# Seeding PSUM with the first half of a product instead of adding it afterwards

## The chip, the cores and the metric

One core of one Trainium2 chip runs the kernel. Its engines work from queues of their own and meet at semaphores: PE (TensorE) multiplies matrices into the PSUM banks, DVE (VectorE) and ACT (ScalarE) do elementwise work and read or write PSUM, POOL (GpSimd) helps with additions, SP (SyncE) issues most DMA transfers. Time is device microseconds of one execution, the median of several; lower is better.

## The reference

One inference step of two trunk layers on 576 tokens (512 of a prompt, 64 of eight sampled sequences), model width 2048, all in float32. Cut to what matters here:

```python
def trunk_layer(x, p, ...):
    h = rmsnorm(x, pre_g)
    proj = h @ w_in                                   # 2048 -> 6144 columns
    u, gp, q, k, v, gr = jnp.split(proj, SPLITS, axis=-1)
    pool_y, buf_new = pool_mixer(u, buf0, ...)        # windows 2, 4, 8, 16, then w_pool
    pool_y = pool_y * silu(gp)
    ret_y, S_new = retention(q.., k.., v.., S0, start)   # rope, 4 heads
    ret_y = head_rmsnorm(ret_y) * silu(gr)
    mix = concatenate([pool_y, ret_y]) @ w_out
    x = x + rmsnorm(mix, post_g)
    ple = rmsnorm(p @ w_ple, ple_g)
    gate = sigmoid(x @ w_ple_gate + b_ple_gate)
    x = x + gate * ple
    return x, S_new, buf_new
```

## The kernel before

**Tiling.** Everything is kept with channels on the 128 partitions and the 576 tokens (`NT`) along the free axis, as two halves of 288 (`HN`), because a PSUM bank holds 512 floats: `half(t, h)` is one half of a tile. A column is one tile of 128 output channels. A float32 product is made of three passes over parts that are split into a high and a low word: `split_part` (L86, L87) makes `wh` on ACT (a cast) and `wl` on DVE (the rest); a column with eight tiles of input is 8 x 3 x 2 = 48 matmuls (L132) into two banks of the four `acc` buffers.

**Two halves of a product.** The input projection and the gate are computed in two halves of the input channels. The first half runs through a Strassen-like scheme (`blocks`, `unit`) whose results go out to DRAM, `proj_dram` and `gate_dram`. The second half is a plain gemm of eight input tiles per column (`gemm`). Its result and the saved first half have to be added: the saved half is loaded into a `part` tile (L451 for the projection, L830 for the gate), DVE adds the two banks to it half by half (L457, L774), and the rest of the work reads the tile.

**The stages that matter.** Per layer: `in_first` (first half of the projection), `in_phase` (its second half, column pairs by `columns(pr)`, then heads of retention and groups of pooling), `out_phase`. The last begins with the output product, then ple, then the gate: its first half by `gate_step`, its second half by the loop at L826 to L835, 16 columns in 8 pairs, which I call the gate's second half. Per column `ct` it loads the saved half, splits the column's weights (two parts, each 128x512), runs the gemm, and calls `gated` (L765 to L786): load of the saved `ple` tile (L767), its scaling on DVE by an STT (scalar_tensor_tensor, L768), two half adds (L774), one sigmoid on ACT over the full width (L776), the product and the residual add on DVE (L777, L778), and a store of the column, `y` in layer 1 (L780), `x` in layer 0 (L782). In layer 0 the loop also squares each column (L314 on ACT, summed on DVE) and, for the first eight columns, scales it for the next layer (L821, in place, so after its store) and splits it again.

**What sets the order.** The code is written column by column; a scheduler lays the instructions of each engine out beforehand and the engines then run their rows strictly in that order, each row waiting for its semaphores. SP's row of DMA issues is one such order: a load that waits holds up all loads behind it. Buffers are rings by tag: `part` has 4, `x` 4 (the ple tiles), `wh` and `wl` 5 each, `raw` (1 MB of weights, one pair of columns) 2. A new tile takes the place of the oldest of its tag and waits for that tile's last reader:

```python
BUFS = {"raw": 2, "wh": 5, "wl": 5, "S": 3, "long": 4, "tmp": 4, "d": 4, "part": 4, "x": 4, "u": 6, ...}
```

So a weight load waits until the last part of the pair two earlier has been split, and a ple load until the residual add of the column four earlier has read its tile.

Of the kernel before, what the change touches and what calls it, by code (L numbers as in the profile page):

```python
# [19 lines left out]
NS = 8  # L20
# [13 lines left out]
def half(ap, h):  # L34
    return ap[:, h * HN:(h + 1) * HN]
# [3 lines left out]
def decoder_kernel(ctx: ExitStack, tc: tile.TileContext, a, decay8):  # L39
# [6 lines left out]
    def buf(tag, shape=(P, NT), dt=F32):  # L46
        return sb.tile(list(shape), dt, tag=tag, name=tag, bufs=BUFS.get(tag, 1))
# [74 lines left out]
    def bank(shape):  # L122
        return ps.tile(list(shape), F32, tag="pb", name="pb", bufs=2)

    def gemm(w, xs, new=acc_tile, by_half=False):
        acc = [new()[:, :HN] for _ in range(2)]
        n = len(w)
        for hs in ((0,), (1,)) if by_half else ((0, 1),):
            for i, ((wh, wl), (xh, xl)) in enumerate(zip(w, xs)):
                for passno, (u, v) in enumerate(((wh, xh), (wh, xl), (wl, xh))):  # L130
                    for h in hs:
                        nc.tensor.matmul(  # L132
                            acc[h], u, v[:, h * HN:(h + 1) * HN],
                            start=(i == 0 and passno == 0), stop=(i == n - 1 and passno == 2),
                        )
        return acc

# [304 lines left out]
    def in_phase(l, raws, r2, rB, cos, sin):  # L442
        b_ring, st_ring, rot_ring, s0_ring = Ring(0, 12), Ring(12, 4), Ring(16, 8), Ring(24, 4)

        def columns(pr):
            keys = [("in2", p) for p in pairs] + [("out", 0, 0), ("out", 0, 1)]
            i = keys.index(("in2", pr))
            raw = raws.pop(("in2", pr))
            for c in range(2):
                t = buf("part")  # L450
                nc.sync.dma_start(out=t, in_=proj_dram[l][2 * pr + c])  # L451
                w = split_weights(raw, 8 * c, 8)
                if c == 1:
                    fetch(l, raws, keys[i + 1:i + 3])
                acc = gemm(w, r2)
                for h in range(2):
                    nc.vector.tensor_tensor(out=half(t, h), in0=acc[h], in1=half(t, h), op=ALU.add)  # L457
                yield t

        def rotary(pr):  # L460
            x = [rot_ring.tile() for _ in range(2)]
            u = [buf("d") for _ in range(2)]
            for i, t in enumerate(columns(pr)):
                nc.vector.tensor_tensor(out=x[i], in0=t, in1=cos, op=ALU.mult)
                nc.vector.tensor_tensor(out=u[i], in0=t, in1=sin, op=ALU.mult)
            nc.vector.tensor_tensor(out=x[0], in0=x[0], in1=u[1], op=ALU.subtract)
            nc.vector.tensor_tensor(out=x[1], in0=x[1], in1=u[0], op=ALU.add)
            return x

        def silu_gates(pr):  # L470
            for t in columns(pr):
                g = buf("g")
                nc.vector.tensor_tensor(out=g, in0=t, in1=rB, op=ALU.mult)
                nc.scalar.activation(g, g, AF.Silu)
                yield g

# [56 lines left out]
        def head(h):  # L533
# [14 lines left out]
            kst = sample_rows(sample_part(k, "kdec_s", h), (0, 2))  # L548

            v = [rot_ring.tile() for _ in range(2)]  # L550
            for i, t in enumerate(columns(16 + h)):
                nc.vector.tensor_tensor(out=v[i], in0=t, in1=rB, op=ALU.mult)
            vt = token_major(v)
            vc = buf("smp", (P, 2, 64))
            for e in range(2):
# [73 lines left out]
        def pool_group(g):  # L629
            w = WINDOWS[g]  # L630
            npool = buf("np", (P, 2, 9, BUF))
            wraw = buf("u", (P, 2, DK))
            nc.sync.dma_start(out=wraw, in_=a["w_pool"][l, g])
            es = buf("u", (P, 2, NB, SEG))
            nc.sync.dma_start(out=es, in_=a["state_pool"][l, :, 2 * g:2 * g + 2])
            wh, wl = buf("u", (P, 2, DK), F32R), buf("u", (P, 2, DK), F32R)
            split(wh, wl, wraw)
            xs = []
            for i, t in enumerate(columns(g)):
                e = buf("d", (P, BUF + NP))  # L640
                nc.vector.memset(e[:, :BUF], 0.0)
                nc.vector.tensor_tensor(out=e[:, BUF:], in0=t[:, :NP], in1=rB[:, :NP], op=ALU.mult)
                nc.vector.tensor_tensor(  # L643
                    out=es[:, i, :, BUF:], in0=t[:, NP:].rearrange("p (b s) -> p b s", s=NS),
                    in1=rB[:, NP:].rearrange("p (b s) -> p b s", s=NS), op=ALU.mult,
                )
                nc.scalar.copy(npool[:, i, 0], e[:, NP:NP + BUF])
                nc.scalar.copy(npool[:, i, 1:], es[:, i, :, NS:])
                s, ss, sh = e, es[:, i], 1
                while sh < w:  # L650
                    n = tmp()[:, :BUF + NP]
                    m = buf("es", (P, NB, SEG))
                    lo = 2 * sh - 1
                    nc.gpsimd.tensor_tensor(out=n[:, lo:], in0=s[:, lo:], in1=s[:, sh - 1:BUF + NP - sh], op=ALU.add)
                    nc.gpsimd.tensor_tensor(out=m[:, :, lo:], in0=ss[:, :, lo:], in1=ss[:, :, sh - 1:SEG - sh], op=ALU.add)  # L655
                    s, ss, sh = n, m, 2 * sh
                p = tmp()
                nc.vector.tensor_tensor(out=p[:, :16], in0=s[:, BUF:BUF + 16], in1=consts["invcnt"][:, g], op=ALU.mult)
                nc.vector.tensor_tensor(out=p[:, :16], in0=p[:, :16], in1=e[:, BUF:BUF + 16], op=ALU.subtract)
                nc.vector.scalar_tensor_tensor(  # L660
                    out=p[:, 16:NP], in0=s[:, BUF + 16:], scalar=1.0 / w, in1=e[:, BUF + 16:], op0=ALU.mult, op1=ALU.subtract
                )
                nc.vector.scalar_tensor_tensor(
                    out=p[:, NP:].rearrange("p (b s) -> p b s", s=NS), in0=ss[:, :, BUF:], scalar=1.0 / w,
                    in1=es[:, i, :, BUF:], op0=ALU.mult, op1=ALU.subtract,
                )
                hi, lo = buf("u", (P, NT), F32R), buf("u", (P, NT), F32R)
                split(hi, lo, p)
                xs.append((hi, lo))
            nc.sync.dma_start(out=a["new_pool"][l, :, 2 * g:2 * g + 2], in_=npool)  # L670
            for c, gate in enumerate(silu_gates(4 + g)):
                acc = gemm([(wh[:, i, c * P:(c + 1) * P], wl[:, i, c * P:(c + 1) * P]) for i in range(2)], xs, mix_tile)
                kt = 2 * g + c
                y = buf("d")
                for i in range(2):
                    nc.vector.scalar_tensor_tensor(
                        out=half(y, i), in0=acc[i], scalar=vec["pool_scale"][:, l, kt:kt + 1], in1=half(gate, i),
                        op0=ALU.mult, op1=ALU.mult,
                    )
                nc.sync.dma_start(out=m_dram[l][kt], in_=y)  # L680
# [16 lines left out]
    def out_phase(l, raws, ops_out):  # L697
# [64 lines left out]
            stats["ss"] = buf("long")  # L762
        rP = buf("long")

        def gated(ct, t, acc, by_half):  # L765
            pl = buf("x")
            nc.sync.dma_start(out=pl, in_=ple_dram[l][ct])  # L767
            nc.vector.scalar_tensor_tensor(  # L768
                out=pl, in0=pl, scalar=vec["ple_g"][:, l, ct:ct + 1], in1=rP, op0=ALU.mult, op1=ALU.mult
            )  # L770
            for hs in ((0,), (1,)) if by_half else ((0, 1),):
                cols = slice(hs[0] * HN, (hs[-1] + 1) * HN)
                for h in hs:
                    nc.vector.tensor_tensor(out=half(t, h), in0=acc[h], in1=half(t, h), op=ALU.add)  # L774
                gate, pc, mc = t[:, cols], pl[:, cols], mo[ct][:, cols]
                nc.scalar.activation(gate, gate, AF.Sigmoid, bias=vec["b_gate"][:, l, ct:ct + 1])  # L776
                nc.vector.tensor_tensor(out=pc, in0=pc, in1=gate, op=ALU.mult)  # L777
                nc.vector.tensor_tensor(out=mc, in0=mc, in1=pc, op=ALU.add)  # L778
                if l == L - 1:
                    nc.sync.dma_start(out=a["y"][:, ct, cols], in_=mc)  # L780
            if l < L - 1:
                nc.sync.dma_start(out=x_dram[ct], in_=mo[ct])  # L782
                square_into(stats["ss"], mo[ct], ct == 0)
# [41 lines left out]
        for p in range(8):  # L825
            raw = raws.pop(("gate2", p))  # L826
            for c in range(2):
                ct = 2 * p + c
                t = buf("part")
                nc.sync.dma_start(out=t, in_=gate_dram[l][ct])  # L830
                w = split_weights(raw, 8 * c, 8)
                if c == 1:
                    fetch_gate(p + 9, p + 11)
                by_half = l == L - 1 and ct == KT - 1
                gated(ct, t, gemm(w, g2, by_half=by_half), by_half)  # L835
            if l < L - 1 and p >= 4:
                blocks(next_xs, [p - 4], next_ops, plain="d")
                if 5 <= p < 7:
# [103 lines left out]
```

## Time and profile before

| | us |
|---|---|
| median of three runs (lowest, highest) | 2267.46 (2265.41, 2268.45) |
| profiled execution, its span | 2264.7 |
| PE busy | 2238.1 |
| DVE busy | 1738.2 |
| ACT busy | 1033.5 |
| gate's second half, layer 0: first column's gemm to last | 1028.8 to 1133.6 |
| gate's second half, layer 1 | 2151.9 to 2258.5 |

The profile is of one execution; no time of that execution other than its span is given, so the span stands for it. Busy time of PE is modelled, and matmuls overlap: one of 128x288 is shown with 0.29 us while the next begins 0.13 us after it. The rows further below show idle time together with the engine or transfer that ended it; the columns are named with each group.

### The profile page before, as it was taken

How to read it: one execution, taken by the hardware profiler on the slowest of the kernel's cores; microseconds unless marked ns; L12 is line 12 of the kernel's file. 1: busy time of each engine (PE TensorE's matmuls, PEld its weight loads, DVE VectorE, ACT ScalarE, POOL GpSimd, SP SyncE). 2: the span in 40 equal slices, each digit the busy share in tenths (PEclk: the TensorE clock that was granted, in tenths of full speed). 3: DMA queues.
4: the chain of work that ended last, by engine and by line, in shares of the span. 5: the costliest groups of instructions: out<-in, count | busy, mean ns of one | idle time of the engine just before them, and what ended most of it. 6: DMA issues, size and time to landing. Idle time of an engine off the chain costs nothing.

```text
span 2264.7 us, 42491 instructions
## 1 busy us (share of the span) xinstructions
PE 2238.1 (99%) x16692; PEld 2153.5 (95%) x16692; DVE 1738.2 (77%) x3141; ACT 1033.5 (46%) x2033; POOL 173.0 (8%) x145
## 2 busy tenths in 40 slices
PE   8999999999999999999999999999999999999998
PEld 8999998898899999899999999988998999998998
DVE  8788766566589898788877786665665989988866
ACT  5465532333334555655545554333333345556532
POOL 2000000000043110000020000000001421100000
PEclk9999999999999999999999999999999999999999
DMA  6455444545343333646644444455454443335564
GB/s 221 151 192 175 156 159 140 174 143 177 127 161 135 130 125 117 215 156 208 222 153 151 164 160 160 145 165 158 135 180 143 148 151 125 115 127 197 174 205 153
DMA packets 137641, 361.92 MB, mean 160 GB/s; under 512 B 14496, under 2 KB 51808, under 8 KB 116576
## 3 DMA queue, kind: packets, MB, share of 16 engines
q1 hardware_dynamic: 137440, 359.20, 47.2%
q8 instruction: 131, 2.15, 0.4%
q14 instruction: 70, 0.57, 0.1%
HBM read 273.10 MB, written 86.04 MB: 159 GB/s over the span
## 4 chain that ended last, share of the span: by engine, by line
PE 81%; DVE 10%; DMA 5%; issue 2%; ACT 1%; SPq 0%; POOL 0%; DVEq 0%; ACTq 0%; POOLq 0%
PE acc L132 27%; PE acc L114 12%; PE acc L113 11%; PE acc L112 11%; PE acc L222 4%; DMA x<-ple 3%; PE pb L113 3%; PE pb L112 3%; PE pb L114 3%; DVE wl L87 2%; PE po L345 2%; PE pb L348 1%; PE po L288 1%; DVE m L87 1%; PE po L132 1%
## 5 line engine op out<-in xcount | busy, mean ns | idle before, releaser
L132 PE MATMUL acc<-m,wh 128*128 128x288 f32 x3584 | 648.6, 297 | 0.0
L86 ACT CAST wh<-raw 128x512 fp32r<-128x512 f32 x567 | 350.7, 619 | 560.6 <-PE acc L132 306.1
L113 PE MATMUL acc<-m,wh 128*128 128x288 f32 x1944 | 573.5, 296 | 0.0
L114 PE MATMUL acc<-m,wl 128*128 128x288 f32 x1944 | 569.0, 296 | 1.8 <-DVE wl L87 1.8
L112 PE MATMUL acc<-m,wh 128*128 128x288 f32 x1944 | 570.7, 295 | 0.0
L132 PEld LDWEIGHTS acc<-m,wh 128*128 128x128 f32 x3584 | 529.5, 188 | 13.2 <-issue 8.8
L87 DVE TENSOR_TENSOR wl<-raw,wh 128x512 fp32r<-128x512 f32 x567 | 409.2, 723 | 121.4 <-ACT wh L86 110.2
L132 PE MATMUL acc<-m,wl 128*128 128x288 f32 x1792 | 401.0, 298 | 0.0
L114 PEld LDWEIGHTS acc<-m,wl 128*128 128x128 f32 x1944 | 363.2, 188 | 2.9 <-DVE wl L87 2.7
L113 PEld LDWEIGHTS acc<-m,wh 128*128 128x128 f32 x1944 | 365.3, 188 | 0.0
L112 PEld LDWEIGHTS acc<-m,wh 128*128 128x128 f32 x1944 | 364.6, 188 | 0.6 <-issue 0.2
L86 ACT CAST wh<-S 128x512 fp32r<-128x512 f32 x356 | 220.6, 620 | 238.1 <-PE acc L113 135.1
L132 PEld LDWEIGHTS acc<-m,wl 128*128 128x128 f32 x1792 | 291.1, 188 | 9.7 <-issue 6.7
L87 DVE TENSOR_TENSOR wl<-S,wh 128x512 fp32r<-128x512 f32 x356 | 252.3, 709 | 29.9 <-ACT wh L86 28.2
L457 DVE TENSOR_TENSOR part<-acc,part 128x288 f32<-128x288 f32 x192 | 79.2, 450 | 64.4 <-PE acc L132 62.8
L235 POOL TENSOR_TENSOR S<-raw 128x512 f32<-128x512 f32 x45 | 67.5, 1499 | 684.4 <-DVE wl L87 316.5
L655 POOL TENSOR_TENSOR es<-u 128x176 f32<-128x176 f32 x16 | 14.5, 908 | 1112.4 <-DVE u L643 1112.2
L235 DVE TENSOR_TENSOR S<-raw 128x512 f32<-128x512 f32 x133 | 91.5, 688 | 9.3 <-DMA raw<-in_w_in 7.2
L349 DVE SCALAR_TENSOR_TENSOR m<-m,pb 128x512 f32<-128x512 f32 x64 | 43.3, 686 | 70.9 <-PE po L345 43.4
L113 PE MATMUL pb<-m,wh 128*128 128x288 f32 x324 | 95.6, 295 | 0.0
L112 PE MATMUL pb<-m,wh 128*128 128x288 f32 x324 | 95.2, 294 | 0.0
L114 PE MATMUL pb<-m,wl 128*128 128x288 f32 x324 | 95.1, 294 | 0.0
(262 smaller groups left out, 3479.6 us busy)
## 6 DMA issues: line engine op xcount, KB each, us to landing
raw<-in_w_in SPq DMA_DIRECT2D x95, 1024.0 KB, 5.3
raw<-in_w_out SPq DMA_DIRECT2D x32, 1024.0 KB, 5.0
raw<-in_w_gate SPq DMA_DIRECT2D x32, 1024.0 KB, 5.5
proj<-d SPq DMA_DIRECT2D x96, 288.0 KB, 2.1
part<-proj SPq DMA_DIRECT2D x96, 288.0 KB, 2.8
m<-in_state_ret SPq DMA_DIRECT2D x64, 256.0 KB, 3.0
out_new_ret_s<-m SPq DMA_DIRECT2D x64, 256.0 KB, 2.8
x<-m SPq DMA_DIRECT2D x48, 288.0 KB, 3.0
```

The lines of the kernel that those rows point to most:

```text
L86: nc.scalar.copy(hi, src)
L87: return nc.vector.tensor_tensor(out=lo, in0=src, in1=hi.bitcast(F32), op=ALU.subtract)
L112: nc.tensor.matmul(out, wh, xh, start=start, stop=False, **kw)
L113: nc.tensor.matmul(out, wh, xl, start=False, stop=False, **kw)
L114: nc.tensor.matmul(out, wl, xh, start=False, stop=stop, **kw)
L132: nc.tensor.matmul(acc[h], u, v[:, h * HN:(h + 1) * HN], start=(i == 0 and passno == 0), stop=(i == n - 1 and passno == 2),)
L222: nc.tensor.matmul(acc[h], w[:, j], xs[h][passno == 1], start=(i == 0 and j == 0 and passno == 0), stop=(i == 1 and j == 3 and passno == 2),)
L235: eng.tensor_tensor(out=s, in0=x, in1=y, op=op)
L288: nc.tensor.matmul(sums[32 * q:32 * q + 32], ones, src[:, q * QN:(q + 1) * QN], start=start, stop=stop)
L345: nc.tensor.matmul(po_s[rows, bg], qrep[:, dt, b * 32:b * 32 + 32], s0[:, dt], start=(dt == 0), stop=(dt == 1))
L349: nc.vector.scalar_tensor_tensor(out=s0, in0=s0, scalar=decay8[h], in1=sp, op0=ALU.mult, op1=ALU.add)
L457: nc.vector.tensor_tensor(out=half(t, h), in0=acc[h], in1=half(t, h), op=ALU.add)
```

## The change

In the second halves of projection and gate, ACT copies the saved half into the two PSUM banks ahead of the gemm (`seed`), and all matmuls add onto that, so the first one no longer overwrites the bank. The half adds on DVE are gone, and the consumers read PSUM: products of the projection (`times`) by halves, the sigmoid by halves with its result in a `part` tile of its own, since the seed's tile is no longer written. That makes two `part` tiles per gate column out of the same ring of 4. Seeds are written at the place where the gemm is called, in program order ahead of its matmuls; the scheduler lays the engines' orders out anew.

```diff
-    def gemm(w, xs, new=acc_tile, by_half=False):
+    def gemm(w, xs, new=acc_tile, by_half=False, seed=None):
         acc = [new()[:, :HN] for _ in range(2)]
+        if seed is not None:
+            for h in range(2):
+                nc.scalar.copy(acc[h], half(seed, h))
...
-                            start=(i == 0 and passno == 0), stop=(i == n - 1 and passno == 2),
+                            start=(seed is None and i == 0 and passno == 0), stop=(i == n - 1 and passno == 2),
+                            skip_group_check=seed is not None,
...
-                acc = gemm(w, r2)
-                for h in range(2):
-                    nc.vector.tensor_tensor(out=half(t, h), in0=acc[h], in1=half(t, h), op=ALU.add)
-                yield t
+                yield gemm(w, r2, seed=t)
+
+        def times(out, acc, row):
+            for h in range(2):
+                nc.vector.tensor_tensor(out=half(out, h), in0=acc[h], in1=half(row, h), op=ALU.mult)
...
-        def gated(ct, t, acc, by_half):
-            pl = buf("x")
+        def gated(ct, acc, by_half):
+            pl, t = buf("x"), buf("part")
...
                 for h in hs:
-                    nc.vector.tensor_tensor(out=half(t, h), in0=acc[h], in1=half(t, h), op=ALU.add)
+                    nc.scalar.activation(half(t, h), acc[h], AF.Sigmoid, bias=vec["b_gate"][:, l, ct:ct + 1])
                 gate, pc, mc = t[:, cols], pl[:, cols], mo[ct][:, cols]
-                nc.scalar.activation(gate, gate, AF.Sigmoid, bias=vec["b_gate"][:, l, ct:ct + 1])
...
-                gated(ct, t, gemm(w, g2, by_half=by_half), by_half)
+                gated(ct, gemm(w, g2, by_half=by_half, seed=t), by_half)
```

In `rotary`, `silu_gates`, the values of a head and `pool_group`, the one product over the full width that read `t` becomes two that read `acc[0]` and `acc[1]` (in `pool_group`, 288 and 224 of the prompt's tokens, and the 64 sampled ones).

The orders of three engines change most in the gate's second half. ACT, layer 1, before: the sigmoid (L776) of a column stands between casts of weight parts (`wh`), and nothing else.

```order
L86 CAST wh_27022<-raw_26750 128x512
L776 ACTIVATE part_26811<-part_26811,c_b_gate_959 128x576
L86 CAST wh_27026<-raw_26750 128x512
L86 CAST wh_27093<-raw_26890 128x512
L776 ACTIVATE part_26880<-part_26880,c_b_gate_959 128x576
```

After, at the start of the same stage; L782 is now the sigmoid and L131 the seed, `part_26754` and `part_26827` are the sigmoids' results of columns 0 and 1, `part_26762` and `part_26835` the saved halves of columns 1 and 2:

```order
L782 ACTIVATE part_26754<-acc_26701,c_b_gate_959 128x288
L782 ACTIVATE part_26754<-acc_26702,c_b_gate_959 128x288
L131 COPY acc_26774<-part_26762 128x288
L131 COPY acc_26775<-part_26762 128x288
L86 CAST wh_26912<-raw_26679 128x512
L86 CAST wh_26981<-raw_26772 128x512
L782 ACTIVATE part_26827<-acc_26774,c_b_gate_959 128x288
L782 ACTIVATE part_26827<-acc_26775,c_b_gate_959 128x288
L131 COPY acc_26845<-part_26835 128x288
L131 COPY acc_26846<-part_26835 128x288
```

The seeds of each column stand directly behind the sigmoids of the column before it.

SP, layer 1, before, from the store of column 0 (`m28`) on: L830 loads a saved half (`gate1` and the column's number), L767 a ple tile, L98 a weight load, L780 stores.

```order
L830 DMA part_26811<-gate14_171 128x576
L780 DMA out_y<-m28_22493 128x576
L767 DMA x_26871<-ple14_139 128x576
L830 DMA part_26880<-gate15_172 128x576
L780 DMA out_y<-m29_22494 128x576
L767 DMA x_26942<-ple15_140 128x576
L830 DMA part_26951<-gate16_173 128x576
L780 DMA out_y<-m30_22593 128x576
L767 DMA x_27011<-ple16_141 128x576
L98 DMA raw_26890<-in_w_gate2 128x2048
```

After (L837 for L830, L775 for L767, L787 for L780):

```order
L837 DMA part_26762<-gate11_168 128x576
L787 DMA out_y<-m28_22653 128x576
L775 DMA x_27041<-ple14_139 128x576
L98 DMA raw_26916<-in_w_gate2 128x2048
L837 DMA part_26835<-gate12_169 128x576
L787 DMA out_y<-m29_22654 128x576
L775 DMA x_27114<-ple15_140 128x576
L837 DMA part_26906<-gate13_170 128x576
L787 DMA out_y<-m30_22753 128x576
L775 DMA x_27185<-ple16_141 128x576
L98 DMA raw_27060<-in_w_gate2 128x2048
L837 DMA part_26979<-gate14_171 128x576
```

Behind the store of column 0 (`m28`) before came the saved half of column 5; now it is that of column 2, and a weight load stands in front of it.

DVE, layer 1, after, between the residual adds of columns 0 and 1 (L785 add, L776 STT, L784 product); the first `wl` here is the last reader of `raw_26679`, whose buffer `raw_26916` takes:

```order
L785 TENSOR_TENSOR m28_22653<-m28_22653,x_26753 128x576
L776 SCALAR_TENSOR_TENSOR x_27041<-x_27041,c_ple_g_957,long_25405 128x576
L87 TENSOR_TENSOR wl_26913<-raw_26679,wh_26912 128x512
L87 TENSOR_TENSOR wl_26982<-raw_26772,wh_26981 128x512
L784 TENSOR_TENSOR x_26826<-x_26826,part_26827 128x576
L785 TENSOR_TENSOR m29_22654<-m29_22654,x_26826 128x576
```

The split that frees the weight buffer stands behind the STT on the ple tile of column 4. Before, this stretch held the two half adds of the next column as well:

```order
L778 TENSOR_TENSOR m30_22593<-m30_22593,x_26731 128x576
L768 SCALAR_TENSOR_TENSOR x_26942<-x_26942,c_ple_g_957,long_25245 128x576
L87 TENSOR_TENSOR wl_26887<-raw_26610,wh_26886 128x512
L774 TENSOR_TENSOR part_26740<-acc_26752,part_26740 128x288
L774 TENSOR_TENSOR part_26740<-acc_26753,part_26740 128x288
L87 TENSOR_TENSOR wl_26954<-raw_26750,wh_26953 128x512
L768 SCALAR_TENSOR_TENSOR x_27011<-x_27011,c_ple_g_957,long_25245 128x576
L777 TENSOR_TENSOR x_26802<-x_26802,part_26740 128x576
L778 TENSOR_TENSOR m31_22594<-m31_22594,x_26802 128x576
```

Only the two L774 rows are gone; the split of a part still stands behind an STT.

In layer 0 ACT has the same pairs of sigmoids and seeds, with the square (L320), the scaling (L828) and its casts between them; `part_13083` is the saved half of column 2:

```order
L782 ACTIVATE part_13072<-acc_13019,c_b_gate_959 128x288
L782 ACTIVATE part_13072<-acc_13020,c_b_gate_959 128x288
L320 ACTIVATE tmp_13080<-m29_8897 128x576
L131 COPY acc_13093<-part_13083 128x288
L131 COPY acc_13094<-part_13083 128x288
L828 ACTIVATE m29_8897<-m29_8897,c_pre_g_279 128x576
L86 CAST m4_13691<-m29_8897 128x576
L86 CAST wh_13239<-raw_13017 128x512
```

Here the square of column 1 stands between its sigmoids and the seeds of column 2.

## Rows read from the trace of the kernel before

**Rows 1.** The page's part 1: engine, busy us, share of the span, instructions.

```profile
PE 2238.1 (99%) x16692; PEld 2153.5 (95%) x16692; DVE 1738.2 (77%) x3141; ACT 1033.5 (46%) x2033; POOL 173.0 (8%) x145
```

**Rows 2.** PE's waits: line, waited for, us in total, times, longest; first and last of nine.

```profile
PE po L132 <- ACT u L86: 7.2, 6, 1.3
...
PE acc L132 <- DVE part L774: 0.2, 1, 0.2
```

**Rows 3.** Windows of the gate's second half, layers 0, 1: length, PE, PEld, DVE, ACT, POOL, PEclk, DMA.

```profile
1046.30:1108.70 62.40, 62.40 (x482) 62.40 (x481) 54.21 (x96) 37.99 (x64) 0.00 (x0) 1.00 0.67 224
2151.90:2233.50 81.60, 81.43 (x622) 81.11 (x622) 53.60 (x90) 27.48 (x45) 0.00 (x0) 1.00 0.62 206
```

**Rows 4.** Costliest groups on DVE, 2160 to 2250 us: busy, mean ns, idle before, releaser.

```profile
L768 DVE SCALAR_TENSOR_TENSOR x<-x,c_ple_g,long 128x576 f32<-128x576 f32 x13 | 10.7, 819 | 29.3 <-DMA x<-ple 29.2
```

**Rows 5.** Timeline of DVE, 2224 to 2231 us: start, us, line, tiles, idle before.

```profile
2223.31 0.76 DVE L778 TENSOR_TENSOR m<-m,x 128x576 f32<-128x576 f32 x1
...
2228.78 0.82 DVE L768 SCALAR_TENSOR_TENSOR x<-x,c_ple_g,long 128x576 f32<-128x576 f32 x1 [2.78 <-DMA x<-ple]
2229.51 0.75 DVE L777 TENSOR_TENSOR x<-x,part 128x576 f32<-128x576 f32 x1
2230.30 0.76 DVE L778 TENSOR_TENSOR m<-m,x 128x576 f32<-128x576 f32 x1
2230.98 0.69 DVE L87 TENSOR_TENSOR wl<-raw,wh 128x512 fp32r<-128x512 f32 x1
```

**Rows 6.** Timeline of SP's issues, 2218 to 2232 us: start, us to issue.

```profile
2225.19 0.40 SPq L98 DMA_DIRECT2D raw<-in_w_gate  x1
```

**Rows 7.** Lines L776 and L245: ns min/median/max, first and last start, forms.

```profile
L776 ACT ACTIVATE part<-part,c_b_gate x33: 534/777/782, 1046.8 to 2260.4; 128x576 f32<-128x576 f32 x31, 128x288 f32<-128x288 f32 x2
...
L245 ACT COPY d<-acc x228: 385/393/404, 39.9 to 2159.6; 128x288 f32<-128x288 f32 x114
```

**Rows 8.** Timeline of the end, PE's last matmul: start, us.

```profile
2258.50 0.29 PE L132 MATMUL acc<-m,wl 128*128 128x288 f32 x1
```

**Rows 9.** Groups on ACT, layer 0, 1060 to 1120 us, forms apart.

```profile
L86 ACT CAST wh<-raw 128x512 fp32r<-128x512 f32 x19 | 11.6, 610 | 0.4 <-PE acc L132 0.4
...
L821 ACT ACTIVATE m<-m,c_pre_g 128x576 f32<-128x576 f32 x6 | 4.7, 779 | 8.7 <-DMA x<-m 8.7
...
L86 ACT CAST d<-m 128x288 fp32r<-128x288 f32 x3 | 1.3, 429 | 0.0
```

**Rows 10.** DMA issues, 1060 to 1125 us: count, KB each, median us from issue to landing.

```profile
raw<-in_w_gate SPq DMA_DIRECT2D x4, 1024.0 KB, 5.5
...
x<-m SPq DMA_DIRECT2D x10, 288.0 KB, 3.2
part<-gate SPq DMA_DIRECT2D x9, 288.0 KB, 2.7
```

**Rows 11.** DMA issues, 685 to 690 us, a saved half issued 0.4 us behind a weight load.

```profile
raw<-in_w_out SPq DMA_DIRECT2D x1, 1024.0 KB, 5.1
part<-proj SPq DMA_DIRECT2D x1, 288.0 KB, 5.5
```

**Rows 12.** Windows of the last microseconds, columns as in rows 3.

```profile
2261.00:2262.00 1.00, 0.00 (x0) 0.00 (x0) 0.84 (x2) 0.00 (x0) 0.00 (x0) 1.00 0.26 90
...
2264.00:2264.70 0.70, 0.00 (x0) 0.00 (x0) 0.00 (x0) 0.00 (x0) 0.00 (x0) 0.50 0.00 0
```

**Rows 13.** Timeline of PE's first matmuls: start, us, idle before.

```profile
6.20 0.61 PE L222 MATMUL acc<-m,wh 128*128 128x288 f32 x1 [6.20 <-ACT wh L86]
...
12.50 0.44 PE L222 MATMUL acc<-tmp,wl 128*128 128x288 f32 x1
12.74 0.40 PE L222 MATMUL acc<-tmp,wh 128*128 128x288 f32 x1
12.97 0.29 PE L222 MATMUL acc<-m,wh 128*128 128x288 f32 x1
```

**Rows 14.** A window in layer 1's pool groups, columns as in rows 3.

```profile
1805.00:1825.00 20.00, 18.42 (x139) 17.96 (x138) 19.21 (x36) 7.62 (x16) 10.81 (x9) 1.00 0.48 157
```

More of the change, by code (lines that the diff above doesn't have):

```diff
@@ L462, in rotary @@
             u = [buf("d") for _ in range(2)]
-            for i, t in enumerate(columns(pr)):
-                nc.vector.tensor_tensor(out=x[i], in0=t, in1=cos, op=ALU.mult)
-                nc.vector.tensor_tensor(out=u[i], in0=t, in1=sin, op=ALU.mult)
+            for i, acc in enumerate(columns(pr)):
+                times(x[i], acc, cos)
+                times(u[i], acc, sin)
             nc.vector.tensor_tensor(out=x[0], in0=x[0], in1=u[1], op=ALU.subtract)
@@ L470, in silu_gates @@
         def silu_gates(pr):
-            for t in columns(pr):
+            for acc in columns(pr):
                 g = buf("g")
-                nc.vector.tensor_tensor(out=g, in0=t, in1=rB, op=ALU.mult)
+                times(g, acc, rB)
                 nc.scalar.activation(g, g, AF.Silu)
@@ L550, in head @@
             v = [rot_ring.tile() for _ in range(2)]
-            for i, t in enumerate(columns(16 + h)):
-                nc.vector.tensor_tensor(out=v[i], in0=t, in1=rB, op=ALU.mult)
+            for i, acc in enumerate(columns(16 + h)):
+                times(v[i], acc, rB)
             vt = token_major(v)
@@ L638, in pool_group @@
             xs = []
-            for i, t in enumerate(columns(g)):
+            for i, acc in enumerate(columns(g)):
                 e = buf("d", (P, BUF + NP))
                 nc.vector.memset(e[:, :BUF], 0.0)
-                nc.vector.tensor_tensor(out=e[:, BUF:], in0=t[:, :NP], in1=rB[:, :NP], op=ALU.mult)
+                nc.vector.tensor_tensor(out=e[:, BUF:BUF + HN], in0=acc[0], in1=rB[:, :HN], op=ALU.mult)
+                nc.vector.tensor_tensor(out=e[:, BUF + HN:], in0=acc[1][:, :NP - HN], in1=rB[:, HN:NP], op=ALU.mult)
                 nc.vector.tensor_tensor(
-                    out=es[:, i, :, BUF:], in0=t[:, NP:].rearrange("p (b s) -> p b s", s=NS),
+                    out=es[:, i, :, BUF:], in0=acc[1][:, NP - HN:].rearrange("p (b s) -> p b s", s=NS),
                     in1=rB[:, NP:].rearrange("p (b s) -> p b s", s=NS), op=ALU.mult,
```

## The prediction

> **What bounds the kernel now.** I read the page's busy time first [rows 1]: PE is busy 99% of the span, DVE 77%, ACT 46%. PE's own waits for other engines come to 20.5 us, the sum of nine lines of the waits view, of which the first and the last stand in [rows 2]. So nothing outside PE can win more than about 20 us, and relieving DVE wins nothing unless PE waits for it. What a change can do is make PE wait. I therefore read next the stage where its edits lie closest to PE, the gate's second half: PE is busy 62.40 of 62.40 us in layer 0 and 81.43 of 81.60 in layer 1 [rows 3]. A matmul begins every 62.40 / 482 = 0.13 us, a column of 48 takes 6.24, and 16 columns follow each other without a gap. That works because nothing PE needs hangs on the column just finished: DVE adds the halves after the gemm (L774), ACT's sigmoid follows, the saved halves are loaded four columns ahead and the weights are split about two ahead.
>
> How little slack there is besides PE shows in layer 1: DVE stands 29.2 us before 13 STTs (L768), for the x<-ple transfer [rows 4]. One turn can be read whole in [rows 5]: the residual add of a column begins at 2223.31, SP may issue the store and the next ple load only behind it, the STT that needs that load begins at 2228.78, the next add at 2230.30. Add to STT 5.5 us, the turn 7.0 against PE's 6.24.
>
> **The change part by part.**
>
> Removed: 256 half-width adds on DVE (L457 192, L774 64), each under the 0.75 us of a full-width product [rows 5]; 128 consumers become two half-width ones. All of it lies beside a full PE; only the last half add is on the tail, which gives under 0.75 us and is left out.
>
> Added: 256 seed copies on ACT. The nearest row is the copy of a half bank the other way, 0.39 us [rows 7]: 101 us, while ACT is busy 1033.5 [rows 1]. As load this costs nothing; its place in three queues does.
>
> *Direct boundary.* ACT's order in the gate is now: a weight cast that waits for gemm c (its buffer is one of five), two sigmoids of column c, two seeds of column c+1, without which gemm c+1 can't start. Two sigmoids of 0.53 and two copies of 0.39 [rows 7], behind the last matmul's own 0.29 [rows 8] and what is left of the cast, some 0.3 of 0.61 [rows 9]; 0.13 of it belongs to the column. So 1.1 + 0.8 + 0.3 + 0.3 - 0.1 = 2.4 us; instructions on one engine overlap a little, I take 2.3. All of it is PE's pause.
>
> *The seed's load.* The saved half of an even column now stands on SP behind the store of the column before the last, the next ple load and the next 1 MB weight load. That weight load waits until DVE has split the last part of the buffer it takes, and this split stands on DVE behind the STT that waits for the ple load. Nobody else can issue: SP waits, the seed's load queues behind it, ACT's seeds behind that, PE behind the seeds. For a pair of columns in layer 1, from add to add of the even ones: 5.5 us from add to STT, 0.7 STT, 0.7 split [rows 5], 0.4 to issue the weight load [rows 6], then the landing of the saved half. Before, such a load lands in 2.7 us, weight loads in 5.5 [rows 10]; where one of the projection's halves was issued directly behind a weight load, it took 5.5 [rows 11], and I take that (bounds 2.7 and 6). Then seeds 0.8, gemm 6.2, 0.5 + 1.1 to the end of the sigmoids, 0.8 for the product before the add. Sum 22.2 us against 2 x 6.24 = 12.5: +9.7 for each of the five even columns with a weight load ahead (2 to 10), 48.5 us. The odd columns between them run beside that; the last five cost the direct boundary, 11.5. Layer 1: **+60 us**.
>
> *Layer 0* has the same queue and a longer way to the split on ACT: the store lands in 3.2 us [rows 10], then ACT scales the column (0.78) and casts it twice (0.43 each) before the weight cast (0.61) [rows 9]. From the add: 0.8 + 3.2 + 0.8 + 0.9 + 0.6 + 0.7 = 7.0 to the end of the split, where layer 1 had 6.9. So +9.7 for columns 2, 4, 6, 8: 39 us. From column 10 on there is no scaling: add 0.8, a square and a cast of the full width (at the scaling's price, 0.8, at most), weight cast 0.6, split 0.7 make some 3.5, the pair 18.8, +6.3 for columns 10, 12, 14: 19. The last column 2.3. Layer 0: **+60 us**.
>
> *TensorE's clock.* In these pairs PE pauses from the end of the odd gemm to the seeds: 22.2 - 12.5 - 2.3 = 7.4 us, nine times, and about 4 us three times. The clock of such pauses can be read at both ends of this trace. At the end the last matmul begins at 2258.50 [rows 8]; the granted clock is still 1.00 in the window up to 2262 and 0.50, the lower level of 1.2 GHz, in the last one [rows 12]. At the start, after 6.2 us without work, matmuls of this width take 0.44 us and begin 0.24 apart up to 12.74, and from 12.97 on 0.29 and 0.13, with 20 matmuls in the slow part [rows 13] (the granted clock is given as 1.00 there, but the spacing is what counts). So each long pause costs 20 x (0.24 - 0.13) = 2.2 us, nine of them **+20 us**; none for the short ones. The Trainium skill has this as a pattern (TensorE: Matmul & The Clock Gate, section "HAM oscillation — how this bites in real kernels"): groups of matmuls parted by waits for transfers each start cold. By it the short pauses could count too, 7 us more.
>
> *The projection's second half.* At the heads, loads stay four columns ahead and PE has other gemms queued: nothing. In the pool groups PE already stands 1.6 of 20 us with DVE near full [rows 14]. There seeds stand on ACT behind small copies (L647, L648) that wait for DVE's products of the column before. Bounds: nothing, if PE has another column queued; two products of 0.75 [rows 5] and two copies of 0.39 [rows 7], 2.3 us for each of 8 columns, 18 a layer. I take 7, nearer to zero because gating columns without such copies lie between: **+14 us**, bounds 0 and 36.
>
> Sum: 60 + 60 + 20 + 14 = +154. The profiled span is 2264.7 us (the last window of [rows 12] ends with it), the median of three runs 2267.46; the 2.8 us between are untouched: **2421 us**.
>
> **The rivals.**
> 1. *Only the direct boundary shows*: weights, ple and saved halves all land before they are needed. 30 boundaries 69 us, in layer 0 seven squares ahead of seeds that wait for product and add, 2.2 each, 15 in all, and 14 as above: +98, 2365 us. For it: with columns further apart, transfers meet less. Against: with a landing of 2.7 instead of 5.5 a pair still takes 19.4 us, 2.3 more than with two direct boundaries.
> 2. *The clock stays low through the gate*: all 48 matmuls after a pause at 0.24, 5.3 us, after all 12 pauses, 64 instead of 20: 2465 us. For it, the pauses come every 22 us. Against, the start recovered within 7 us of work.
> 3. *Faster*: DVE is relieved, and part of PE's 20.5 us of waits [rows 2] goes: 0 to -20, say 2255 us. It decides for itself if the seeds of column c+1 stand ahead of column c's sigmoids on ACT and their load ahead of the store; then PE never waits. In the order they stand behind in every gate column, so I give it little.
> 4. *Nothing to measure*: gains and losses cancel within 0.2% (4.5 us, about what a measurement of this kernel can tell from no change), as if the seeds were hidden and the 20.5 us stayed.
>
> **How the numbers follow.** The forecast gets 0.62; its own spread is 2385 (saved halves at 2.7 on half the pairs, pool groups 0) to 2445 (pool groups at their upper bound). Rival 1 0.13, rival 2 0.18, rival 3 0.04, rival 4 0.03. The range takes the forecast, most of what lies between it and rival 1, and rival 2 short of its end: 2368 to 2460. Faster 0.03, same 0.04, slower 0.93.
>
> **What would show it.** PE's gaps in the changed kernel's gate: about 7 us before columns 2, 4, 6, 8 (and 10 in layer 1), ended by ACT's seed, with the seed in turn waiting for the load part<-gate; 2.3 us before odd ones. SP's load right behind a weight load, landing at 5 to 6 us. Matmuls at 0.24 for 2 to 5 us after each long gap. 2.3 us gaps alone are rival 1; no gaps rival 3; if the projection's second half loses time at the heads, I missed a queue.

## The result, and the profile after

| | before | after |
|---|---|---|
| median (lowest, highest), us | 2266.43 (2264.12, 2268.45), 4 runs | 2419.07 (2414.6, 2421.16), 4 runs |
| span of the profiled execution, us | 2264.7 | 2419.0 |

Ratio 1.0676, 95% interval 1.0662 to 1.069: the change costs 153 us. The forecast was 2421. The page's busy time, which answers to [rows 1]:

```profile
PE 2281.1 (94%) x16692; PEld 2191.0 (91%) x16692; DVE 1652.0 (68%) x3013; ACT 1130.9 (47%) x2320; POOL 156.0 (6%) x145
```

PE's work is the same; it is spread over 154 us more. DVE lost 86 us of work and ACT gained 97, and neither shows in the time. The waits of PE, which were 20.5 us in [rows 2], are headed by one that did not exist (line, waited for, us in total, times, longest); the second is the one at the kernel's start and belongs to both kernels:

```profile
PE acc L137 <- ACT acc L131: 116.3, 35, 8.1
PE acc L228 <- ACT wh L86: 6.4, 1, 6.4
```

**Where the time lies.** Both kernels run 16,692 matmuls, so the start of the n-th can be set beside the start of the n-th. The shift is -0.1 us up to the projection's second half, +6.0 when the gate of layer 0 begins, +83.2 behind it, +90.8 when the gate of layer 1 begins, and +155.9 at the last matmul. So the two projections cost 6.0 and 7.6 us, the two gates 77.1 and 65.2. Behind the last matmul the kernel needs 4.6 us where it needed 6.2, so the spans differ by 154.3. Windows of the gate's second half from its second column on, which answer to [rows 3], and two short ones in layer 0 (length; busy us of PE, PEld, DVE, ACT, POOL; PEclk; DMA share; GB/s):

```profile
1051.50:1211.90 160.40, 108.14 (x671) 105.14 (x672) 72.18 (x106) 60.17 (x118) 1.26 (x1) 0.85 0.37 124
2259.40:2411.40 152.00, 110.01 (x697) 106.78 (x698) 48.95 (x67) 36.33 (x82) 0.00 (x0) 0.87 0.34 115
1082.60:1090.00 7.40, 0.29 (x3) 0.05 (x1) 3.48 (x5) 2.51 (x6) 0.00 (x0) 0.86 0.79 269
1090.00:1094.50 4.50, 4.46 (x18) 4.46 (x19) 1.58 (x2) 1.77 (x3) 0.00 (x0) 0.50 0.14 53
```

PE stands still for 33% and 28% of the first two. The third window is one pause, and in the fourth, right behind it, the granted clock is 0.50, the lower level of 1.2 GHz. What happens around that pause, in the timeline (start, us, instruction, idle before):

```profile
1080.96 0.82 DVE L776 SCALAR_TENSOR_TENSOR x<-x,c_ple_g,long 128x576 f32<-128x576 f32 x1 [1.95 <-DMA x<-ple]
...
1082.43 0.68 DVE L87 TENSOR_TENSOR wl<-raw,wh 128x512 fp32r<-128x512 f32 x1
...
1083.14 0.33 SPq L98 DMA_DIRECT2D raw<-in_w_gate  x1
...
1083.57 0.38 SPq L837 DMA_DIRECT2D part<-gate  x1
...
1084.89 0.76 DVE L785 TENSOR_TENSOR m<-m,x 128x576 f32<-128x576 f32 x1
...
1089.59 0.73 ACT L131 COPY acc<-part 128x288 f32<-128x288 f32 x2 [3.22 <-DMA part<-gate]
...
1098.55 0.62 ACT L86 CAST wh<-raw 128x512 fp32r<-128x512 f32 x1 [1.48 <-PE acc L137]
1099.08 0.89 ACT L782 ACTIVATE part<-acc,c_b_gate 128x288 f32<-128x288 f32 x2
...
1099.85 0.74 ACT L131 COPY acc<-part 128x288 f32<-128x288 f32 x2
```

This is the queue of the forecast, row by row: the STT waits for its ple load; the split behind it ends at 1083.11; only then is the weight load issued, and the saved half behind it; the seeds wait 3.2 us for that half and begin at 1089.59; PE begins at 1090.04. The last three rows are the next boundary, the direct one: weight cast, two sigmoids, two seeds. How PE starts behind the long pause (rows of two or three matmuls show the time of all):

```profile
1090.04 0.85 PE L137 MATMUL acc<-u,wh 128*128 128x288 f32 x2 [7.16 <-ACT acc L131]
1090.69 0.44 PE L137 MATMUL acc<-u,wl 128*128 128x288 f32 x1
...
1094.29 0.44 PE L137 MATMUL acc<-m,wl 128*128 128x288 f32 x1
...
1095.05 0.29 PE L137 MATMUL acc<-u,wl 128*128 128x288 f32 x1
```

Matmuls of 0.44 us begin 0.24 apart, as in [rows 13]; from 1094.77 on they begin 0.13 apart again, 0.29 long. And the two transfers issued there, at 1083.14 and 1083.57 (count, KB each, us from issue to landing), to be set beside the 2.7 us of [rows 10]:

```profile
raw<-in_w_gate SPq DMA_DIRECT2D x1, 1024.0 KB, 5.1
part<-gate SPq DMA_DIRECT2D x1, 288.0 KB, 6.0
```

The twelve saved halves that are issued 0.4 us behind a weight load took 5.0 to 6.0 us, 5.4 in the mean, and landed 0.7 to 1.3 us behind it; the others in the two gates took 3.0 to 5.5.

### The profile page after: what moved, and what is told of

The parts are those of the page before. It is cut to its first block, busy times and chain, and to the rows that moved or that the text cites. A ratio compares the mean times of both kernels' runs of the same rounds, so it can differ in the third digit from the quotient of the medians.

```text
span 2419.0 us, 42651 instructions
## 1 busy us (share of the span) xinstructions
PE 2281.1 (94%) x16692; PEld 2191.0 (91%) x16692; DVE 1652.0 (68%) x3013; ACT 1130.9 (47%) x2320; POOL 156.0 (6%) x145
## 4 chain that ended last, share of the span: by engine, by line
PE 92%; DMA 3%; ACT 2%; DVE 2%; issue 1%; SPq 0%; ACTq 0%; DVEq 0%
PE acc L137 37%; PE acc L112 12%; PE acc L113 12%; PE acc L114 12%; PE acc L228 4%; PE pb L113 3%; DMA part<-gate 3%; PE pb L112 3%; PE pb L114 3%; PE po L351 2%; PE pb L354 1%; PE po L137 1%; PE po L294 1%; ACT part L782 1%; PE po L312 1%
## 5 line engine op out<-in xcount | busy, mean ns | idle before, releaser
L137 PE MATMUL acc<-m,wh 128*128 128x288 f32 x3584 | 683.5, 301 | 19.4 <-ACT acc L131 16.1
L137 PEld LDWEIGHTS acc<-m,wh 128*128 128x128 f32 x3584 | 550.3, 192 | 36.3 <-ACT acc L131 17.6
L113 PE MATMUL acc<-m,wh 128*128 128x288 f32 x1944 | 573.0, 295 | 0.0
L112 PE MATMUL acc<-m,wh 128*128 128x288 f32 x1944 | 570.9, 295 | 0.5 <-ACT m L251 0.5
L114 PE MATMUL acc<-m,wl 128*128 128x288 f32 x1944 | 567.0, 295 | 0.0
L137 PE MATMUL acc<-m,wl 128*128 128x288 f32 x1792 | 421.0, 300 | 0.0
L112 PEld LDWEIGHTS acc<-m,wh 128*128 128x128 f32 x1944 | 364.4, 188 | 1.9 <-ACT m L251 1.0
L113 PEld LDWEIGHTS acc<-m,wh 128*128 128x128 f32 x1944 | 365.0, 188 | 0.0
L114 PEld LDWEIGHTS acc<-m,wl 128*128 128x128 f32 x1944 | 362.6, 188 | 0.2 <-DVE wl L87 0.2
L137 PEld LDWEIGHTS acc<-m,wl 128*128 128x128 f32 x1792 | 302.2, 191 | 7.1 <-issue 4.6
L137 PE MATMUL acc<-u,wh 128*128 128x288 f32 x384 | 95.8, 345 | 100.2 <-ACT acc L131 100.2
L137 PEld LDWEIGHTS acc<-u,wh 128*128 128x128 f32 x384 | 73.7, 227 | 106.9 <-ACT acc L131 106.9
L131 ACT COPY acc<-part 128x288 f32<-128x288 f32 x256 | 100.3, 402 | 84.0 <-DMA part<-gate 33.8
```

The source lines that it names most:

```text
L112: nc.tensor.matmul(out, wh, xh, start=start, stop=False, **kw)
L113: nc.tensor.matmul(out, wh, xl, start=False, stop=False, **kw)
L114: nc.tensor.matmul(out, wl, xh, start=False, stop=stop, **kw)
L131: nc.scalar.copy(acc[h], half(seed, h))
L137: nc.tensor.matmul(acc[h], u, v[:, h * HN:(h + 1) * HN], start=(seed is None and i == 0 and passno == 0), stop=(i == n - 1 and passno == 2 ...
```

## The experiments

The theory had four parts: a direct boundary, the seed's load in SP's queue, the clock, and pauses in the projection. The runs take them apart one by one. Kernels are compared with the kernel before on the same chip (its median there was 2264 to 2266 us).

**One stage at a time.** Only the projection seeded, `gated` as before:

> Seeds in the projection's second half only; the gate adds on DVE as before. Theory (both stages lose, each for itself): the shift of the matmuls at the end of the two in-phases, 6.0 and 7.6 us, comes alone: 2266 + 14 = 2280 us. Rival (the whole loss is the gate's, the shift in the projection is only an echo of the other instruction order): 2266 us.

Measured 2278.7 us, ratio 1.0059 (1.0044 to 1.0074). Only the gate seeded, `columns` and its consumers as before:

> Seeds in the gate's second half only; the projection adds on DVE as before. Theory: the changed kernel less the projection's 14 us, 2405 us, with the same pauses of 5 to 8 us at even columns. Rival (the two parts help each other to be slow, by the seeds' orders on ACT): clearly under 2400 us.

Measured 2407.2, ratio 1.0625 (1.061 to 1.0641). The two parts add up within 4 us: 14 and 142 against 153 together. Each stage loses for itself.

**The seed's load out of SP's queue.**

```diff
-                nc.sync.dma_start(out=t, in_=gate_dram[l][ct])
+                nc.gpsimd.dma_start(out=t, in_=gate_dram[l][ct])
```

> The changed kernel, with only the 32 loads of the gate's saved halves issued by POOL, whose queue is empty there, and not by SP; the orders of ACT and DVE stay as they are but for a dozen rows. Theory (the seed's load waits in SP's queue behind store, ple load and weight load): the pauses of 5.4 to 8.4 us at even columns fall to 1.8 us in layer 1 and about 4 us in layer 0, where the square stands ahead of the seeds; the time to about 2362 us. Rival (the buffer ring or ACT's order holds the seeds, not the queue): no change, 2419 us, and POOL's load issued as late as SP's was.

Measured 2372.8, ratio 1.0479 (1.0463 to 1.0494). The pauses before the even columns of layer 1 are now at most 1.83 us from one matmul's start to the next, like those before odd ones; in layer 0 they are 4.1 to 5.9. The transfers issued around 2292 us, one more load around 2300 us, and the window of columns 1 to 15 of layer 1:

```profile
raw<-in_w_gate SPq DMA_DIRECT2D x1, 1024.0 KB, 5.5
part<-gate POOLq DMA_DIRECT2D x1, 288.0 KB, 5.9
```

```profile
part<-gate POOLq DMA_DIRECT2D x1, 288.0 KB, 3.2
```

```profile
2248.30:2370.20 121.90, 101.09 (x720) 97.86 (x720) 48.73 (x71) 36.31 (x83) 7.01 (x13) 0.98 0.43 142
```

A load is no quicker for being POOL's: issued 0.3 us behind a weight load it took 5.9 us, issued when none was under way 3.2. What changed is that no store, ple load or weight load stands ahead of it, so it is issued earlier against the seeds that need it. In the changed kernel five seeds of layer 1 waited for their load (idle us of ACT, times, longest):

```profile
ACT acc L131 <- DMA part<-gate: 20.7, 5, 4.6
```

Here none of them does, and PE is busy 101 of 122 us where it was 110 of 152. So the queue is shown: 46 us of the loss go with hardly anything changed but who issues 32 loads. But by the starts of the matmuls 33 us of this are layer 1's (its gate loses 32 instead of 65) and only 11 layer 0's (66 instead of 77). There the seeds of an even column then wait for the square, and the square for DVE's residual add:

```profile
1084.22 0.88 ACT L782 ACTIVATE part<-acc,c_b_gate 128x288 f32<-128x288 f32 x2
1086.72 0.68 ACT L320 ACTIVATE tmp<-m 128x576 f32<-128x576 f32 x1 [1.62 <-DVE m L785]
1087.31 0.72 ACT L131 COPY acc<-part 128x288 f32<-128x288 f32 x2
```

What is left is the direct boundary, in layer 0 the square ahead of the seeds, and the clock behind the long pauses; behind a direct boundary of 1.83 us the matmuls keep their 0.13.

**The ring.** The sigmoid's result gets a ring of its own:

```diff
-            pl, t = buf("x"), buf("part")
+            pl, t = buf("x"), buf("tmp")
```

> The changed kernel, with the sigmoid's result in a ring of its own (4 tiles of the tag tmp) and not in that of the saved halves. In the built order the loads run four columns ahead again and most seeds stand ahead of the sigmoids of the column before. Theory (two tiles a column out of one ring of four made both the late load and the late seed): the gate's loss goes, 2266 + 14 = 2280 us, the projection's loss stays. Rival (the seeds on ACT cost PE a pause at every boundary wherever they stand): 30 boundaries of 1.7 us, 2330 us.

Measured 2280.2, ratio 1.0067 (1.0051 to 1.0084), the projection's loss and 1.5 us. ACT in layer 1, and a window of 80 us there:

```profile
2203.56 0.89 ACT L782 ACTIVATE tmp<-acc,c_b_gate 128x288 f32<-128x288 f32 x2
2204.34 0.73 ACT L131 COPY acc<-part 128x288 f32<-128x288 f32 x2
```

```profile
2186.00:2266.00 80.00, 80.00 (x602) 80.00 (x601) 42.09 (x61) 31.82 (x72) 0.00 (x0) 1.00 0.55 187
```

The pair of copies behind the sigmoids is still there, but PE doesn't wait for it: by their count in the trace these are the sigmoids of column 4 and the seeds of column 6. PE is busy 80.00 of 80.00 us; ahead of this window one pause of 1.8 us a layer is left, before column 2. So nearly the whole of the gate's loss came from two tiles a column drawn from one ring of four, which led to an order in which load and seed come late; a seed costs PE nothing when it stands a column ahead.

**The clock.** First try: matmuls into an unread bank behind the odd columns.

```diff
+                if c == 1 and (p < 7 if l < L - 1 else p < 5):
+                    fill = bank((P, 512))
+                    for _ in range(38):
+                        nc.tensor.matmul(fill[:, :HN], g2[0][0][:, :P], g2[0][0][:, :HN], start=True, stop=True)
```

> The changed kernel, with 38 further matmuls of 288 columns (4.9 us at 0.13) behind each odd gate column that a long pause follows, into a PSUM bank that nobody reads; nothing is left out. They lie inside the pauses of 5.4 to 8.4 us, so they move no other work. Theory (the slow half columns are TensorE's clock, fallen in the pause): the matmuls at 0.24 behind the filled pauses go, 12 pauses by 2.1 us, 25 us: 2394 us. Rival (the slow spacing is the start of a gemm on freshly seeded banks, or its weights): no gain, 2419 us.

Measured 2432.8, ratio 1.0744 (1.0729 to 1.0759). The run is inconclusive: the added matmuls depend on nothing late, so PE's order has them before, inside and between the first columns, and the pauses behind these stay empty. The second try reads the weight part whose split ends as the pause begins (`w[7][1]`), in pairs 1 to 7 of layer 0 and 1 to 5 of layer 1, 34 times each:

> The changed kernel, with 34 further matmuls (4.4 us) into an unread PSUM bank between each odd gate column and the even one behind it, 12 places; they read a weight part that is split just before the weight load is issued, so PE's order can't pull them ahead of the pause as in the run before. Nothing is left out. Theory (the clock falls in the pause): PE starts the even columns warm, 12 times 2.1 us: 2394 us, and no 0.24 spacing behind filled pauses. Rival (the slow half column comes from the fresh seed or the weights, or the fill only displaces): 2419 us or more, 0.24 spacing unchanged.

Measured 2399.7, ratio 1.0592 (1.0576 to 1.0608): 408 more matmuls, and 19 us faster than without. PE behind a filled pause of layer 0, and the two gates' windows (columns as above):

```profile
1087.02 0.53 PE L137 MATMUL acc<-u,wh 128*128 128x288 f32 x2 [2.05 <-ACT acc L131]
1087.39 0.30 PE L137 MATMUL acc<-u,wl 128*128 128x288 f32 x1
```

```profile
1052.00:1198.80 146.80, 127.63 (x910) 123.93 (x909) 71.86 (x106) 59.93 (x117) 1.26 (x1) 0.98 0.40 135
2245.00:2390.00 145.00, 123.75 (x890) 120.50 (x890) 50.04 (x69) 36.99 (x84) 0.00 (x0) 0.98 0.36 122
```

The matmuls begin 0.13 apart from the second on, and the clock is 0.98 where it was 0.85 and 0.87. Of the 12 even columns behind a filled pause 11 start so; one, with 2.1 us left open before it, has 15 slow matmuls from its 11th on, and the columns behind unfilled pauses of 3.3 us have 16 and 21. The 12 pauses, fills included, are as long as they were (76 us in sum, 75 before), so the gain isn't from shorter pauses. The clock is shown as the cause; the seeds' banks and the weights were the same.

**The projection.** There the profile after put the blame on a bank. ACT's seeds (us idle before them, times, by releaser), and the place, where the last head passes into the first pool group:

```profile
  DMA part<-gate: 33.8, 12
  DVE d L465: 24.6, 50
  DVE g L465: 14.4, 6
```

```profile
627.84 3.36 DVE L620 TENSOR_TENSOR m<-m,tmp 128x576 f32<-128x576 f32 x2
...
633.73 0.81 DVE L465 TENSOR_TENSOR g<-acc,long 128x288 f32<-128x288 f32 x2
634.21 0.40 ACT L131 COPY acc<-part 128x288 f32<-128x288 f32 x1 [5.14 <-DVE g L465]
```

A seed waits 5.1 us for a SiLU gate's product to free its bank, and that product stands in DVE's queue behind two products of 1.7 us each. Before, the half adds freed the banks. So the SiLU gates were left unseeded, with the sigmoid's own ring, then only those of the pool groups, then with the gate phase as before too:

```diff
-            for acc in columns(pr):
+            for t in columns(pr, False):          # gemm, then the two half adds
                 g = buf("g")
-                times(g, acc, rB)
+                nc.vector.tensor_tensor(out=g, in0=t, in1=rB, op=ALU.mult)
```

> The changed kernel with the sigmoid's own ring, and the 16 SiLU gate columns of each layer's projection unseeded (half adds on DVE as before); heads' and pool inputs stay seeded. Theory (the projection's loss is one pause of 6.8 us a layer in which ACT's seed waits for a bank that a gate product, far back in DVE's queue, still reads, and what trails it): the pause goes, the small gains in the pool groups stay: 2280 - 19 = 2261 us, under the kernel before. Rival (ACT's casts that wait for PE hold the seeds up): the pause moves to another seed, 2275 to 2280 us.

> As the run before, but only the 8 gate columns of the pool groups are unseeded, the 8 of the heads stay seeded. Theory: the pause stands where the last head passes into the first pool group, and the product that held the bank there was a pool group's gate, so this too removes it: 2261 us. Rival (it is a head's gate): 2280 us.

> Seeds only for the heads' and pool inputs of the projection; SiLU gates and the gate phase as before. Theory: as the gate with its own ring gave no gain, the same time as with it, 2261 us. Rival (the gate's lighter DVE is worth something): 2 to 4 us slower than the run with the gate seeded.

Measured 2281.6, 2281.6 and 2280.7 (ratios 1.0076, 1.0076, 1.0075, each about 0.0015 either way). The theory fell: in none of them a seed waits for a SiLU gate's bank any more, but a pause nearly as long (6.6 us, in the second run 5.7 to 5.9) stands a little later, before the first pool product. So the remaining seeds were taken apart, with the gate phase and SiLU gates as before: only the heads' q, k and v, and only the pool inputs.

> Seeds only for the heads' q, k and v columns (48 of 96 in number of halves); pool inputs, SiLU gates and the gate as before. Theory A (the pause at the passage from the last head to the first pool group comes from the pool inputs' seeds): the pause is gone and what the heads gain by then, 2 to 3 us a layer, stays: 2259 us. Theory B (it comes from the heads' own seeds, which change the order there): the pause stays, 2278 us.

> Seeds only for the pool inputs (16 half copies a layer); heads, SiLU gates and the gate as before. Theory A (pool inputs' seeds make the pause): 2275 to 2280 us, with a pause of 6 us or more near 636 us. Theory B (the heads' seeds make it): 2262 to 2264 us.

Measured 2261.0, ratio 0.9979 (0.997 to 0.9988), and 2285.5, ratio 1.0082 (1.0069 to 1.0096). The heads' seeds alone make the kernel faster than before, by 0.2%; the pool inputs' alone cost more than the whole projection did. The last run seeds all but the pool inputs:

> The changed kernel with both faults taken out: the sigmoid's own ring, and the 8 pool input columns of each layer unseeded; heads, SiLU gates and the gate phase stay seeded. Theory (the ring made the gate's loss, the pool inputs' seeds the projection's): the kernel with the heads alone seeded, 2261 us, plus the 1.5 us that the seeded gate with its own ring cost: 2262 us, no pause over 2.5 us behind the last head. Rival (the SiLU gates' seeds make a pause there too): 2272 us or more.

Measured 2280.5, ratio 1.0072 (1.0058 to 1.0085): missed. With the SiLU gates seeded the pause is back. The same 40 us of layer 0 in before, after, heads alone, pool inputs alone and all but the pool inputs, in this order (columns as above):

```profile
620.00:660.00 40.00, 38.79 (x293) 38.48 (x294) 35.09 (x70) 14.62 (x29) 17.09 (x14) 1.00 0.47 171
```

```profile
620.00:660.00 40.00, 32.72 (x228) 32.25 (x227) 31.91 (x64) 15.87 (x35) 15.53 (x15) 0.87 0.48 160
```

```profile
620.00:660.00 40.00, 40.00 (x306) 39.85 (x305) 36.89 (x68) 15.14 (x30) 16.47 (x14) 1.00 0.46 155
```

```profile
620.00:660.00 40.00, 29.50 (x201) 27.65 (x193) 32.03 (x62) 13.48 (x29) 16.86 (x15) 0.83 0.46 147
```

```profile
620.00:660.00 40.00, 30.98 (x218) 30.56 (x219) 31.87 (x62) 13.99 (x29) 16.85 (x16) 0.87 0.33 110
```

PE loses 6 to 9 us here in every kernel that seeds either the pool inputs or the SiLU gates, and the half clock behind the pause adds to it. With pool inputs alone it waits for the pool tile itself, which ACT casts after DVE and POOL have made it; with SiLU gates it waits for the bank that a gate's product reads:

```profile
PE po L137 <- ACT u L86: 17.5, 5, 6.9
```

```profile
PE acc L137 <- DVE g L471: 13.8, 2, 7.0
```

In the first case 54 projection matmuls stand in PE's order between the last head's sums and the first pool product, in the kernel before 94. So either kind of seed changes what PE has to do in a stretch in which DVE is busy 32 to 37 of 40 us. Why the order there comes out shorter was not separated: no run held the order fixed and changed the seeds alone.

## Why the prediction was right

The time was right (2421 against 2419), and so was the mechanism that carries most of it. The terms, from the gaps between matmul starts less the 0.13 that belongs to them:

| term | forecast | measured |
|---|---|---|
| 12 long pauses before even columns | 79 | 74 |
| direct boundaries, gate | 41 | 37 |
| half clock in the gate | 20 | 31 |
| projection | 14 | 14 |
| sum | 154 | 156 |

The gates' three measured terms come to 142, as the shift of their matmuls does (77.1 + 65.2). That the sum is off by 2 only is luck in part: the pauses and boundaries were 9 too high, the clock 11 too low. The 156 are those of the last matmul; the end behind it became 1.6 us shorter, where the forecast had put under 0.75 and left it out.

- *Long pauses.* Right in place, cause and nearly in size: 5.3 to 8.2 us, with the saved half landing 5.0 to 6.0 us after its issue behind the weight load (forecast 5.5). In layer 0, columns 10 to 14 paused 5.3 to 5.5 where 4 was forecast, and column 2 in both layers 5.3 where 7.4 was. The forecast laid layer 0's pauses to the load alone. The pool-queue run shows a second hold there, nearly as long, the square ahead of the seeds, which the forecast had only in its first rival, at 2.2 us a time.
- *Direct boundary.* 1.70 us and not 2.3. Two sigmoids take 0.89 together and two seeds 0.74, and the gemm begins at 1100.32, before the second seed (which began after 1099.85) is done: only the first bank's seed is on the path. But the first boundary of each layer cost 3.2, with the sigmoid's table load of 1.3 us now on the path, and the first column 2.0 more in pauses inside it, neither of which the forecast had.
- *Clock.* The price of 2.2 us a pause was right. Its condition was too narrow: it struck not nine pauses of 7 us but all 14 of 3.3 us and more, with 12 to 25 slow matmuls each, and the pauses of 5 us as much as those of 8. The sentence from the Trainium skill (TensorE: Matmul & The Clock Gate, "HAM oscillation — how this bites in real kernels"), by which the short pauses count too, was nearer to it than the forecast's own reading of the last microseconds.
- *Projection.* Right number, wrong step: luck. The forecast had 7 us a layer in small pauses of pool columns behind ACT's copies, and nothing at the heads. It was one pause of 6.8 us a layer at the passage from the last head, with slow matmuls behind it. Three pauses of about 1 us shortly ahead of it cost 2 us, the pause and what trails it 9 to 10, and the pool groups behind it gave 5.8 and 3.6 back. Two errors cancelled.
- *Rivals.* The pool-queue run comes close to the first rival made real: 2373 against its 2365. The second (clock low throughout) is out, the clock is back after 12 to 25 matmuls. The third was right in its condition: with seeds a column ahead PE does not wait. But what it then wins in the gate is nil. The forecast's own spread, 2385 to 2445, comes to 2390 and 2443 by its terms, which changes nothing.

## What to carry to other kernels

Moving work to an idle engine changes three orders, the engine's own and those of the DMA queue and the buffers: read for each new instruction what stands in front of it there, and price the queue, not the instruction. A second tile from a ring of four cost 139 us here; with a ring of its own the same code lost 1.5 us in the gate. And on a TensorE that is full, a pause costs its length and, behind all pauses of 3.3 us and more in the changed kernel's gates, 1.4 to 2.9 us in slow matmuls.

## What the runs showed that was not expected

- The clock was at its lower level for 16 to 25 matmuls behind pauses of 3.3 us, and with the pauses filled by 34 matmuls it stayed up though 0.9 to 2.4 us of each were still open behind the fill (one of twelve fell). In the heads-alone run it fell for some 14 matmuls, 1.6 us behind a pause of 2.1 before a pool product.
- A 288 KB load issued 0.4 us behind a 1 MB load took 5.0 to 6.0 us and landed just behind it. From POOL's queue, issued within 1.7 us of one, it took 5.7 to 6.5 (four loads of layer 1), so another queue did not make it faster.
- Taking 86 us of work from DVE won nothing; seeding the heads alone, 48 columns of two layers, won 4.7 us (0.2%).
